# Output projection as seven half-size products (Strassen's scheme in Winograd's form) in a hybrid encoder layer

## The chip, the core and the metric

The kernel runs on one core of a Trainium2 chip. A core has five engines that run side by side, each in its own order, and wait for each other by semaphores: TensorE (PE; its weight loads are shown apart as PEld), VectorE (DVE), ScalarE (ACT), GpSimd (POOL) and SyncE (SP), which here issues all transfers between DRAM and the on-chip memory SBUF. TensorE writes its sums into PSUM, eight banks of 128 x 512 float32. The metric is the device time of one execution in microseconds (us); lower is better.

## What is computed

One layer on x of 2048 tokens by 2048 channels, float32. The condition c gives shift, scale and gate; the normalised input goes through one projection to 4096 columns; half the width is mixed by centred pooling windows, half by a recurrent unit in both directions; each half is normalised, gated and projected back, and the sum with x is normalised.

```python
mod = c_act @ w_ada[l] + b_ada[l]
shift, scale, gate = jnp.split(mod, 3, axis=-1)
h = rms_norm(x, norm_g[l]) * (1.0 + scale[:, None, :]) + shift[:, None, :]
z = h @ w_in[l] + b_in[l]
...
y_pool = rms_norm(y_pool, out_norm_pool_g[l]) * jax.nn.silu(g_pool)
y_lru = rms_norm(y_lru, out_norm_lru_g[l]) * jax.nn.silu(g_lru)
y = jnp.concatenate([y_pool, y_lru], axis=-1) @ w_out[l] + b_out[l]
x = x + gate[:, None, :] * y
return rms_norm(x, final_norm_g)
```

## The kernel before

All large products are made in two parts per operand: a float32 value is split into a rounded part and the rest (`m_split`, `w_split`, `y_split`: ScalarE copies, VectorE subtracts), and `mm3` adds three of the four part products. The work is a list of steps t. A step takes one moving operand M (256 rows of the sum by 512 columns, two parts) against four stationary tiles of 128, two halves of the sum and three part products: 24 matmuls into four PSUM banks.

Steps 0 to 255 are the input projection: eight groups of 256 channels, four token blocks of 512 each, eight steps to a sum. Beside them, at steps given by `at(step, function, ...)`, run the mixers of the groups that are ready (`lru_unit`, `pool_unit`), which leave y in DRAM (`yscr`) and the sums of squares of each half in `sq`; `rn` turns these into 1/rms.

Steps 256 to 383 are the output projection (`where2`): four token blocks (tb), four blocks of 512 output columns (dc), eight pairs p of 128 rows each. The y of a token block is loaded (`y_load`), multiplied by 1/rms and split (`y_split`) once, and stays in the eight buffers of pool `s` for the four column blocks. The blocks of w_out come in as M, one per step. When a sum is complete, `out_evac` multiplies the bank by the gate row, adds it to the row tile o (which holds x plus gate times b_out) and squares it; when all four column blocks are there, `out_row` makes 1/rms of the row, multiplies and stores.

What sets the order: the loop over t issues, for step t, the loads four steps ahead (`m_load`, `AHEAD`), the split of the operand for step t+2, the split of one w or y operand, the products of step t, then whatever `at` holds for t. The framework then orders the instructions of each engine by its own estimate, so the written order on VectorE is not the order of the code. Buffers come from pools that are used in turn: `raw` has 7 buffers for everything that is loaded and split, `m` has 3, `s` has 8; a load into a buffer waits on SP's queue until the buffer's last reader is done, and all loads behind it wait too. In the last four steps the products go tile by tile, so that a row's end can start while the next tile is still being summed.

```python
    def m_split(t):
...
        act(out=m[:, 0], in_=r, func=AF.Copy)
        vtt(out=m[:, 1], in0=r, in1=mf[:, 0], op=ALU.subtract)
```

## Time and profile before

| | |
|---|---|
| median of 3 runs | 2354.26 us (2354.2 to 2354.26) |
| span of the profiled execution, first to last instruction | 2352.7 us |
| granted TensorE clock, mean | 0.998 |
| PE, PEld, DVE, ACT, POOL busy | 99%, 82%, 65%, 54%, 0% |
| bytes moved | 437.09 MB, 186 GB/s on average |

The profiled execution has no run time of its own beside its span; the runs are 1.6 us longer than the span. The page gives busy shares of each engine, the same in 40 slices of the span, and the chain of work that ended last. The views of the trace list what an engine waited for, the mean duration of each group of instructions, the busy time in a stretch, and instructions in order of time. The input projection fills the span up to 1635 us, the output projection the rest.

### The profile page before, as it was taken

How to read it: one execution, taken by the hardware profiler on the slowest of the kernel's cores; microseconds unless marked ns; L12 is line 12 of the kernel's file. 1: busy time of each engine (PE TensorE's matmuls, PEld its weight loads, DVE VectorE, ACT ScalarE, POOL GpSimd, SP SyncE). 2: the span in 40 equal slices, each digit the busy share in tenths (PEclk: the TensorE clock that was granted, in tenths of full speed). 3: DMA queues.
4: the chain of work that ended last, by engine and by line, in shares of the span. 5: the costliest groups of instructions: out<-in, count | busy, mean ns of one | idle time of the engine just before them, and what ended most of it. 6: DMA issues, size and time to landing. Idle time of an engine off the chain costs nothing.

```text
span 2352.7 us, 26479 instructions
## 1 busy us (share of the span) xinstructions
PE 2330.4 (99%) x10216; PEld 1917.9 (82%) x10216; DVE 1524.7 (65%) x1898; ACT 1261.5 (54%) x1609; POOL 6.2 (0%) x40
## 2 busy tenths in 40 slices
PE   7999999999999999999999999999999999999998
PEld 6888888888888888888888888888788888888886
DVE  7999676567877555574764756569936636637535
ACT  4556686767656665665776566675323224224222
POOL 0000000000000000000000000000000000000000
PEclk9999999999999999999999999999999999999999
DMA  9889755345565634444363344446534634625531
GB/s 390 310 303 324 253 208 199 112 170 215 215 242 210 219 116 145 142 154 137 135 241 116 130 143 157 157 166 229 221 97 161 250 99 152 252 98 198 196 97 74
DMA packets 110655, 437.09 MB, mean 186 GB/s; under 512 B 12224, under 2 KB 13504, under 8 KB 100544
## 3 DMA queue, kind: packets, MB, share of 16 engines
q1 hardware_dynamic: 110528, 435.40, 52.0%
q8 instruction: 80, 1.31, 0.2%
q14 instruction: 47, 0.39, 0.1%
HBM read 358.80 MB, written 76.55 MB: 185 GB/s over the span
## 4 chain that ended last, share of the span: by engine, by line
PE 98%; DMA 1%; DVE 0%; SPq 0%; ACT 0%; issue 0%; DVEq 0%
PE pm L249 25%; PE pm L247 25%; PE pm L248 25%; PE px L247 7%; PE px L249 7%; PE px L248 7%; DMA ada<-in_wada_dram 1%; PE px L330 0%; DMA xr<-in_xc_dram 0%; PE px L644 0%; DVE ada L315 0%; DVE o L671 0%; SPq L274 0%; SPq L273 0%; PE px L212 0%; ACT s L225 0%
## 5 line engine op out<-in xcount | busy, mean ns | idle before, releaser
L247 PE MATMUL pm<-m,s 128*128 128x512 f32 x2638 | 1031.7, 391 | 0.0
L249 PE MATMUL pm<-m,s 128*128 128x512 f32 x2638 | 1027.0, 389 | 0.0
L248 PE MATMUL pm<-m,s 128*128 128x512 f32 x2638 | 1026.9, 389 | 0.0
L156 DVE TENSOR_TENSOR m<-xr,m 128x1024 fp32r<-128x1024 f32 x382 | 465.7, 1220 | 562.9 <-ACT m L155 557.7
L155 ACT ACTIVATE m<-xr 128x1024 fp32r<-128x1024 f32 x382 | 403.7, 1057 | 765.5 <-PE pm L249 607.7
L248 PEld LDWEIGHTS pm<-m,s 128*128 128x128 f32 x2638 | 495.4, 188 | 105.9 <-issue 2.2
L247 PEld LDWEIGHTS pm<-m,s 128*128 128x128 f32 x2638 | 495.3, 188 | 105.6 <-issue 2.6
L249 PEld LDWEIGHTS pm<-m,s 128*128 128x128 f32 x2638 | 495.2, 188 | 103.5
L247 PE MATMUL px<-m,s 128*128 128x512 f32 x426 | 164.6, 393 | 12.9 <-ACT m L296 12.5
L248 PE MATMUL px<-m,s 128*128 128x512 f32 x426 | 164.2, 391 | 0.0
L249 PE MATMUL px<-m,s 128*128 128x512 f32 x426 | 164.0, 391 | 0.0
L315 DVE CUSTOM_DVE_ANT_0 ada<-ada,cact 128x2048 f32<-128x2048 f32 x47 | 107.4, 2284 | 10.1 <-DMA ada<-in_wada_dram 10.1
L247 PEld LDWEIGHTS px<-m,s 128*128 128x128 f32 x426 | 80.1, 189 | 30.7 <-ACT m L296 12.5
L247 PE MATMUL px<-uch,gw 128*128 128x512 f32 x256 | 100.7, 394 | 0.0
L249 PE MATMUL px<-uch,gw 128*128 128x512 f32 x256 | 100.7, 393 | 0.0
L248 PE MATMUL px<-uch,gw 128*128 128x512 f32 x256 | 99.5, 389 | 0.0
L248 PEld LDWEIGHTS px<-m,s 128*128 128x128 f32 x426 | 80.4, 189 | 17.3 <-DVE m L297 0.4
L249 PEld LDWEIGHTS px<-m,s 128*128 128x128 f32 x426 | 80.4, 189 | 16.7
L476 DVE SCALAR_TENSOR_TENSOR th<-rg,th 128x512 f32<-128x512 f32 x64 | 42.7, 682 | 77.7 <-ACT th L471 77.6
L457 DVE TENSOR_TENSOR ig<-ig,u 128x512 f32<-128x512 f32 x64 | 44.2, 691 | 66.3 <-ACT ig L455 66.2
L656 ACT ACTIVATE ov<-o 128x512 f32<-128x512 f32 x64 | 39.9, 624 | 68.1 <-DVE o L655 68.1
L221 DVE TENSOR_TENSOR s<-wr,s 128x1024 fp32r<-128x1024 f32 x56 | 68.1, 1215 | 0.0
(166 smaller groups left out, 2069.2 us busy)
## 6 DMA issues: line engine op xcount, KB each, us to landing
xr<-xs SPq DMA_DIRECT2D x192, 512.0 KB, 4.8
xr<-in_wout_dram SPq DMA_DIRECT2D x128, 512.0 KB, 3.7
ada<-in_wada_dram SPq DMA_DIRECT2D x47, 1024.0 KB, 7.0
wr<-in_win_dram SPq DMA_DIRECT2D x71, 512.0 KB, 5.5
xr<-in_xc_dram SPq DMA_DIRECT2D x63, 512.0 KB, 6.1
gs<-gr SPq DMA_DIRECT2D x32, 512.0 KB, 3.1
xs<-xr SPq DMA_DIRECT2D x32, 512.0 KB, 3.7
gl<-gs SPq DMA_DIRECT2D x32, 512.0 KB, 3.5
```

Source lines behind the costliest of these rows:

```text
L155: act(out=m[:, 0], in_=r, func=AF.Copy)
L156: vtt(out=m[:, 1], in0=r, in1=mf[:, 0], op=ALU.subtract)
L221: vtt(out=s[:, 1], in0=r, in1=sf[:, 0], op=ALU.subtract)
L247: nc.tensor.matmul(out=ps, lhsT=a[:, 0, j, asl], rhs=b[:, 0, j], start=first, stop=False)
L248: nc.tensor.matmul(out=ps, lhsT=a[:, 0, j, asl], rhs=b[:, 1, j], start=False, stop=False)
L249: nc.tensor.matmul(out=ps, lhsT=a[:, 1, j, asl], rhs=b[:, 0, j], start=False, stop=last)
L315: nc.vector.tensor_tensor_reduce(out=t, in0=t, in1=cact["t"], op0=ALU.mult, op1=ALU.add, scale=1.0, scalar=0.0, accum_out=mod[:, i:i + 1])
L457: vtt(out=st["i", i], in0=st["i", i], in1=U[i][:, us], op=ALU.mult)
L476: stt(out=t, in0=a, scalar=1.0, in1=t, op0=ALU.add, op1=ALU.mult)
L656: act(out=v, in_=o[:, ds], func=AF.Square, accum_out=ssq[:, 4 * tb + t, dc:dc + 1])
```

## The change

The output projection is made by Strassen's scheme with Winograd's seven products. 1024 tokens (a group sg, two token blocks) by 2048 rows of the sum by 2048 columns are cut into halves in each direction: A11, A12, A21, A22 are the quarters of y (first index the token block, second the half of the channels) and B11 to B22 those of w_out. The products are A11 B11, A12 B21, S2 T2, S3 T3, A22 T4, S1 T1 and S4 B22, with S1 = A21 + A22, S2 = S1 - A11, S3 = A11 - A21, S4 = A12 - S2 and T1 = B12 - B11, T2 = B22 - T1, T3 = B22 - B12, T4 = T2 - B21. Each product has two column blocks q of 512 and four pairs p, 8 steps; a group has 56 steps and there are two groups, so the steps 256 to 367 stand where 256 to 383 stood. A step is the same 24 matmuls.

The combinations T1 to T4 are made during the input projection (`combine_load`, `combine`, `combine_store`, 32 times) and kept in DRAM. The quarters of y are loaded one unit after the other (`unit_load`, `unit_split`, one unit every two steps from step 249 on); a normalised quarter is written back to DRAM and loaded again where it is needed. `out_evac` copies or adds each product's bank into the tiles of `C_t`; product 1 is added onto the bank of product 0, and product 6 onto that of product 5, after these have been read (`CHAINED`). x is loaded in half rows (`x_load`), gate and b_out come in afterwards (`half_fin`, `part_fin`). `raw` has 8 buffers; the pools of the mixers are closed at step 262 and the rows of gate, b_out and final norm take their place. Comments were removed in the same edit.

```diff
-    raw_p = pool("raw", 7)
+    raw_p = pool("raw", 8)
...
+    mix_pools = [tc.alloc_tile_pool(name=n, bufs=b, side="right") for n, b in (("tmp", 9), ("gw", 1), ("uch", 1))]
+    tmp_p, gw_p, uch_p = mix_pools
...
+    tscr = [[[dram.tile([128, 2, TB], F32, name=f"t{k}_{p}_{q}") for q in range(2)] for p in range(4)] for k in range(4)]
+    sscr = [dram.tile([128, 2, TB], F32, name=f"ss{p}") for p in range(4)]
...
     NT1 = 256
-    NT = 384
+    SG = 56
+    NT = NT1 + 2 * SG
...
+    PRODUCTS = [("A11", "B11"), ("A12", "B21"), ("S2", "T2"), ("S3", "T3"), ("A22", "T4"), ("S1", "T1"), ("S4", "B22")]
+    CHAINED = {1: 0, 6: 5}
     def where2(t):
-        """Token block, column block, pair of a step of the output projection."""
-        i = t - NT1
-        return i // 32, i // 8 % 4, i % 8
-
-    # ---- operands: the exact two-part split of float32 ----
+        sg, i = divmod(t - NT1, SG)
+        return sg, i // 8, i // 4 % 2, i % 4
+    def wout_src(name, p, q):
+        k = int(name[1:])
+        if name[0] == "T":
+            return tscr[k - 1][p][q]
+        return wout[p + 4 * (k // 10 - 1), q + 2 * (k % 10 - 1)]
     S_t = {}
...
-            tb, dc, p = where2(t)
-            load(out=r, in_=wout[p, dc])
+            sg, k, q, p = where2(t)
+            load(out=r, in_=wout_src(PRODUCTS[k][1], p, q))
...
+    def combine_load(k, p, q):
...
+        a, b = (("B12", "B11"), ("B22", "T1"), ("B22", "B12"), ("T2", "B21"))[k]
+        for i, n in enumerate((a, b)):
+            r = raw("tr")
+            load(out=r, in_=wout_src(n, p, q))
+            wraw["t", k, i] = r
+    def combine(k, p, q):
+        a, b = wraw.pop(("t", k, 0)), wraw.pop(("t", k, 1))
+        vtt(out=a, in0=a, in1=b, op=ALU.subtract)
+        wraw["t", k] = a
+    def combine_store(k, p, q):
+        store(out=tscr[k][p][q], in_=wraw.pop(("t", k)))
...
+    def unit_args(u):
+        sg, u = divmod(u, 28)
+        return sg, PRODUCTS[u // 4][0], u % 4
+    def unit_load(u):
+        sg, name, p = unit_args(u)
+        ya, yb = ([yscr[PAIRS[k]][2 * sg + h] for k in (p, p + 4)] for h in range(2))
+        srcs = {"A11": [ya[0]], "A12": [ya[1]], "S2": [yb[0], yb[1], ya[0]], "S3": [ya[0], yb[0]], "A22": [yb[1]],
+                "S1": [yb[0], yb[1]], "S4": [ya[1], sscr[p]]}[name]
+        yraw[u] = []
+        for src in srcs:
+            r = raw("yr")
+            load(out=r, in_=src)
+            yraw[u].append(r)
+    def normed(r, sg, h, k, p):
+        for j in range(2):
+            vtt(out=r[:, j], in0=r[:, j], in1=rn_t[2 * sg + h, "PL"[k]], op=ALU.mult)
+        late.append((yscr[PAIRS[p + 4 * k]][2 * sg + h], r))
+        if (sg, h, p) == (0, 1, 3):
+            del rn_t[1, "PL"[k]], rn_t[0, "PL"[k]]
+    def unit_split(u):
+        sg, name, p = unit_args(u)
+        rs = yraw.pop(u)
+        r = rs[0]
+        if name in ("A11", "A12"):
+            normed(r, sg, 0, int(name[2]) - 1, p)
+        elif name == "S2":
+            r = rs[2]
+            normed(rs[0], sg, 1, 0, p)
+            normed(rs[1], sg, 1, 1, p)
+            vtt(out=r, in0=r, in1=rs[0], op=ALU.subtract)
+            vtt(out=r, in0=rs[1], in1=r, op=ALU.subtract)
+            late.append((sscr[p], r))
+        elif name in ("S3", "S4"):
+            vtt(out=r, in0=r, in1=rs[1], op=ALU.subtract)
+        elif name == "S1":
+            vtt(out=r, in0=r, in1=rs[1], op=ALU.add)
         s = s_p.tile([128, 2, 2, TB], F32R, tag="s", name="s")
-        sf = s.bitcast(F32)
-        rn = sq[GROUPS[PAIRS[p]][0]][:, tb * TB:(tb + 1) * TB]
-        for j in range(2):
-            vtt(out=r[:, j], in0=r[:, j], in1=rn, op=ALU.mult)
         act(out=s[:, 0], in_=r, func=AF.Copy)
-        vtt(out=s[:, 1], in0=r, in1=sf[:, 0], op=ALU.subtract)
-        S_t[8 + tb, p] = s
...
+    def mm3(ps, a, asl, b, j, first, last, more=False):
+        for i, (x, y) in enumerate(((0, 0), (0, 1), (1, 0))):
+            nc.tensor.matmul(out=ps, lhsT=a[:, x, j, asl], rhs=b[:, y, j], start=first and i == 0, stop=last and i == 2,
+                             skip_group_check=more)
...
+    def step(bk, sk, p, m, tiles, first, last, by_j=False, more=False):
...
+    def rows_open():
...
+        for p in reversed(mix_pools):
+            p.release()
+        row_p = ctx.enter_context(tc.tile_pool(name="row", bufs=1, side="right", reuse_waits="tile"))
+        for n in ("gb", "fg", "gate"):
+            fin[n] = row_p.tile([128, D], F32, tag=n, name=n)
...
+        for i, (tb, kind) in enumerate([(2, "P"), (2, "L"), (3, "P"), (3, "L")]):
+            act(out=fin["rn"][:, i], in_=rn_t[tb, kind], func=AF.Copy)
+            rn_t[tb, kind] = fin["rn"][:, i]
+        sq.clear()
...
+    def out_evac(sg, k, q, banks, tiles):
+        lo, hi = (slice((q + 2 * h) * TB, (q + 2 * h + 1) * TB) for h in range(2))
+        for n in tiles:
+            for i, at_k in ((n, 0), (n + 4, 3)):
+                if k == at_k and q == 0:
+                    C_t[sg, i] = big("o")[:, :D]
+            a, b, ps = C_t[sg, n], C_t.get((sg, n + 4)), banks[n]
+            if k == 0:
+                act(out=a[:, hi], in_=ps, func=AF.Copy)
+            elif k == 1:
+                act(out=a[:, lo], in_=ps, func=AF.Copy)
+            elif k in (2, 6):
+                vtt(out=a[:, hi], in0=ps, in1=a[:, hi], op=ALU.add)
+            elif k == 3:
+                vtt(out=b[:, hi], in0=ps, in1=a[:, hi], op=ALU.add)
+            elif k == 4:
+                vtt(out=b[:, lo], in0=b[:, hi], in1=ps, op=ALU.subtract)
+            else:
+                vtt(out=b[:, hi], in0=ps, in1=b[:, hi], op=ALU.add)
...
+        x_t[sg, n, h] = r
+    def x_add(sg, n, h):
+        r = x_t[sg, n, h]
+        vtt(out=r, in0=r, in1=fin["gb"][:, h * 1024:(h + 1) * 1024], op=ALU.add)
+    def part_fin(sg, n, h, lo, hi, slot):
+        r = x_t[sg, n, h][:, lo:hi]
+        ds = slice(h * 1024 + lo, h * 1024 + hi)
+        o = C_t[sg, n][:, ds]
+        vtt(out=o, in0=o, in1=fin["gate"][:, ds], op=ALU.mult)
+        vtt(out=o, in0=o, in1=r, op=ALU.add)
+        act(out=r, in_=o, func=AF.Square, accum_out=ssq[:, row_of(sg, n), slot:slot + 1])
+        if hi == 1024:
+            del x_t[sg, n, h]
+    def half_fin(sg, n, h):
+        x_add(sg, n, h)
+        part_fin(sg, n, h, 0, 1024, h)
+    def out_row(sg, n, slots, parts):
+        i = row_of(sg, n)
+        o = C_t.pop((sg, n))
         s = ssq[:, i]
         r = rst[:, i:i + 1]
-        vtt(out=s[:, 0:1], in0=s[:, 0:1], in1=s[:, 1:2], op=ALU.add)
-        vtt(out=s[:, 0:1], in0=s[:, 0:1], in1=s[:, 2:3], op=ALU.add)
...
+    for i in range(32):
+        q, k = divmod(i, 4)
+        b = 68 + 5 * i if i < 7 else 134 + (i - 7) * 9 // 2
+        at(b, combine_load, k, q // 2, q % 2)
+        at(b + 2, combine, k, q // 2, q % 2)
+        at(b + 3, combine_store, k, q // 2, q % 2)
...
+    for sg in range(2):
+        b = NT1 + SG * sg
+        for n in range(4):
+            step_b = (49 + 2 * n, 49 + n)[sg]
+            for i, h, e in ((n, 0, b + 22 + 2 * n), (n + 4, 0, b + 41 + 2 * n), (n + 4, 1, b + step_b)):
+                at(e - 2, x_load, sg, i, h)
+                at(e, half_fin, sg, i, h)
+            at(b + 50 + n, x_load, sg, n, 1)
+            if sg == 0:
+                at(b + 52 + n, x_add, sg, n, 1)
+                at(b + 56 + n, part_fin, sg, n, 1, 0, 1024, 1)
+                at(b + 56 + n, out_row, sg, n, 2, 1)
+                at(b + 61 + n, out_row, sg, n + 4, 2, 1)
+            else:
+                at(b + 50 + n, out_row, sg, n + 4, 2, 1)
+                e = b + min(52 + n, 54)
+                at(e, x_add, sg, n, 1)
+                at(e, part_fin, sg, n, 1, 0, TB, 1)
...
+    rn_at = [(244, 1, "L"), (244, 2, "L"), (245, 3, "L"), (245, 0, "P"), (249, 1, "P"), (250, 0, "L"), (254, 2, "P"), (259, 3, "P")]
...
+    unit_at = {}
+    for u in range(56):
+        unit_at[max(NT1 - 10 + 2 * u, NT1 - 7 + u)] = u
...
-            key = (8 + tb, dc)
-            sk = 8 + tb
+            sg, k, q, p = where2(t)
+            key = (8 + sg, CHAINED.get(k, k), q)
+            sk = (8 + sg, PRODUCTS[k][0])
...
+        for dst, src in late:
+            store(out=dst, in_=src)
+        late.clear()
...
+        if t + W_AHEAD in unit_at:
+            unit_load(unit_at[t + W_AHEAD])
...
+        if t in unit_at:
+            unit_split(unit_at[t])
...
-                out_evac(tb, dc, bk, range(4))
-                if dc == 3:
-                    for i in range(4):
-                        at(t + 2 + i, out_row, tb, i, 1)
+                out_evac(sg, k, q, bk, range(4))
             else:
                 for i in range(4):
-                    for q in range(4, 8):
-                        step(bk, sk, q, M_t[t - 7 + q], (i,))
-                    out_evac(tb, dc, bk, (i,))
-                    out_row(tb, i, 4 if i == 3 else 2)
-        # the rest
```

On VectorE, at the border of two token blocks before (splits for steps 323 to 325): m is the moving operand, s and yr the operand made of y, o a row tile, `fg` the row of the final norm.

```order
L156 TENSOR_TENSOR m_14252<-xr_14164,m_14252 128x1024
L242 TENSOR_TENSOR s_14255<-yr_14166,s_14255 128x1024
L665 TENSOR_TENSOR rst_101<-ssq_100 128x1 x4
L667 RECIPROCAL rst_101<-rst_101 128x1
L671 SCALAR_TENSOR_TENSOR o_13285<-o_13285,rst_101,fg_12049 128x2048
L156 TENSOR_TENSOR m_14290<-xr_14200,m_14290 128x1024
L667 RECIPROCAL rst_101<-rst_101 128x1 x3
L671 SCALAR_TENSOR_TENSOR o_13324<-o_13324,rst_101,fg_12049 128x2048
L671 SCALAR_TENSOR_TENSOR o_13363<-o_13363,rst_101,fg_12049 128x2048
L156 TENSOR_TENSOR m_14326<-xr_14250,m_14326 128x1024
L671 SCALAR_TENSOR_TENSOR o_13395<-o_13395,rst_101,fg_12049 128x2048
```

and at the border of the two token groups in the changed kernel (splits for steps 320 and 321), where `rn` holds 1/rms, and the three yr are the quarters of an S2 operand:

```order
L170 TENSOR_TENSOR m_14627<-xr_14539,m_14627 128x1024
L280 TENSOR_TENSOR yr_14542<-yr_14542,rn_12524 128x512
L280 TENSOR_TENSOR yr_14544<-yr_14544,rn_12524 128x512 x2
L295 TENSOR_TENSOR yr_14546<-yr_14546,yr_14542 128x1024
L769 TENSOR_TENSOR rst_101<-ssq_100 128x1
L296 TENSOR_TENSOR yr_14546<-yr_14544,yr_14546 128x1024
L771 RECIPROCAL rst_101<-rst_101 128x1
L775 SCALAR_TENSOR_TENSOR o_13329<-o_13329,rst_101,fg_12520 128x2048
L304 TENSOR_TENSOR s_14636<-yr_14546,s_14636 128x1024
L170 TENSOR_TENSOR m_14673<-xr_14584,m_14673 128x1024
```

The row normalisations by `fg` stood next to each other between splits and now stand among the products and differences of the S2 operand, nine rows between two splits.

On VectorE, the end before, from the bank of the third tile on (px and pm are PSUM banks):

```order
L654 TENSOR_TENSOR ov_16379<-px_16162,gate_12051 128x512
L655 TENSOR_TENSOR o_15571<-o_15571,ov_16379 128x512
L665 TENSOR_TENSOR rst_101<-ssq_100 128x1
L667 RECIPROCAL rst_101<-rst_101 128x1
L671 SCALAR_TENSOR_TENSOR o_15571<-o_15571,rst_101,fg_12049 128x1024 x2
L654 TENSOR_TENSOR ov_16416<-pm_16163,gate_12051 128x512
L655 TENSOR_TENSOR o_15603<-o_15603,ov_16416 128x512
L665 TENSOR_TENSOR rst_101<-ssq_100 128x1
L667 RECIPROCAL rst_101<-rst_101 128x1
L671 SCALAR_TENSOR_TENSOR o_15603<-o_15603,rst_101,fg_12049 128x512 x4
```

and the end of the changed kernel, from the bank of the fourth tile on:

```order
L725 TENSOR_TENSOR o_14530<-pm_16036,o_14530 128x512
L775 SCALAR_TENSOR_TENSOR o_14526<-o_14526,rst_101,fg_12520 128x1024 x2
L769 TENSOR_TENSOR rst_101<-ssq_100 128x1
L753 TENSOR_TENSOR o_14530<-o_14530,gate_12521 128x512
L771 RECIPROCAL rst_101<-rst_101 128x1
L769 TENSOR_TENSOR ssq_100<-ssq_100 128x1
L754 TENSOR_TENSOR o_14530<-o_14530,x_16341 128x512
L775 SCALAR_TENSOR_TENSOR o_14528<-o_14528,rst_101,fg_12520 128x1024 x2
L769 TENSOR_TENSOR rst_101<-ssq_100 128x1
L771 RECIPROCAL rst_101<-rst_101 128x1
L775 SCALAR_TENSOR_TENSOR o_14530<-o_14530,rst_101,fg_12520 128x512 x4
```

Before, a tile's half rows (L671) stood ahead of the next tile's bank; now the half rows of the second and third tile (L775 on o_14526 and o_14528) stand behind the bank of the fourth.

## Rows read from the trace of the kernel before

**Rows 1.** Page: busy time and share by engine, and the granted clock in 40 slices.
```profile
PE 2330.4 (99%) x10216; PEld 1917.9 (82%) x10216; DVE 1524.7 (65%) x1898; ACT 1261.5 (54%) x1609; POOL 6.2 (0%) x40
...
PEclk9999999999999999999999999999999999999999
```
**Rows 2.** Waits of TensorE: who waited for whom, us in total, times, longest.
```profile
PE px L247 <- ACT m L296: 12.5, 1, 12.5
```
**Rows 3.** Page: the chain that ended last, by engine.
```profile
PE 98%; DMA 1%; DVE 0%; SPq 0%; ACT 0%; issue 0%; DVEq 0%
```
**Rows 4.** Timeline of VectorE late in the kernel: start us, us, line, operation, tiles.
```profile
2284.42 1.23 DVE L156 TENSOR_TENSOR m<-xr,m 128x1024 fp32r<-128x1024 f32 x1 [4.21 <-ACT m L155]
2289.86 1.23 DVE L156 TENSOR_TENSOR m<-xr,m 128x1024 fp32r<-128x1024 f32 x1 [4.21 <-ACT m L155]
```
**Rows 5.** Timeline of ScalarE, same stretch; in brackets idle before, and its end.
```profile
2310.58 1.06 ACT L155 ACTIVATE m<-xr 128x1024 fp32r<-128x1024 f32 x1 [4.38 <-PE pm L249]
```
**Rows 6.** Groups of VectorE by line and shape: busy, mean ns, idle before.
```profile
L156 DVE TENSOR_TENSOR m<-xr,m 128x1024 fp32r<-128x1024 f32 x382 | 465.7, 1220 | 562.9 <-ACT m L155 557.7 <-DMA o<-in_xn_dram 4.2 <-issue 0.3
...
L671 DVE SCALAR_TENSOR_TENSOR o<-o,rst,fg 128x2048 f32<-128x2048 f32 x12 | 27.9, 2348 | 0.1
...
L240 DVE TENSOR_TENSOR yr<-yr,sqL 128x512 f32<-128x512 f32 x32 | 21.1, 686 | 20.7 <-DMA yr<-ys 20.7
...
L240 DVE TENSOR_TENSOR yr<-yr,sqP 128x512 f32<-128x512 f32 x32 | 20.7, 686 | 26.9 <-DMA yr<-ys 26.9
...
L332 DVE RECIPROCAL sqP<-sqP 128x512 f32<-128x512 f32 x4 | 13.4, 3346 | 0.8 <-ACT sqP L331 0.8
```
**Rows 7.** Timelines of VectorE and TensorE around the start of step 266.
```profile
1692.74 1.28 DVE L655 TENSOR_TENSOR o<-o,ov 128x512 f32<-128x512 f32 x2
...
1699.60 2.29 DVE L156 TENSOR_TENSOR m<-xr,m 128x1024 fp32r<-128x1024 f32 x2
...
1701.05 0.62 PE L247 MATMUL px<-m,s 128*128 128x512 f32 x2
```
**Rows 8.** Stretches: busy us of PE, PEld, DVE, ACT, POOL; clock, DMA share, GB/s.
```profile
1635.00:2321.00 686.00, 686.00 (x3009) 564.46 (x3009) 380.19 (x438) 208.39 (x297) 0.00 (x0) 1.00 0.46 160
...
1657.16:1700.75 43.59, 43.59 (x181) 33.77 (x180) 43.29 (x28) 13.77 (x21) 0.00 (x0) 1.00 0.47 180
...
0.00:40.00 40.00, 27.09 (x106) 21.25 (x107) 28.29 (x39) 18.49 (x21) 0.44 (x6) 1.00 0.97 378
```
**Rows 9.** Chain of waits in order of time: the sum over partitions for 1/rms.
```profile
1604.31 0.86 PE px L330 x2
```
**Rows 10.** Transfers by tiles: count, KB each, median us from issue to landing.
```profile
xr<-in_xc_dram SPq DMA_DIRECT2D x63, 512.0 KB, 6.1
...
yr<-ys SPq DMA_DIRECT2D x32, 512.0 KB, 3.3
```
**Rows 11.** Waits of SP's queue: us in total, times, longest.
```profile
SPq L140 <- DVE m L156: 359.4, 77, 16.2
```
**Rows 12.** Timeline of VectorE at the end, from the last tile's bank on.
```profile
2340.82 2.48 DVE L671 SCALAR_TENSOR_TENSOR o<-o,rst,fg 128x1024 f32<-128x1024 f32 x2
2343.39 0.69 DVE L654 TENSOR_TENSOR ov<-pm,gate 128x512 f32<-128x512 f32 x1
2344.12 0.69 DVE L655 TENSOR_TENSOR o<-o,ov 128x512 f32<-128x512 f32 x1
2345.59 0.16 DVE L665 TENSOR_TENSOR rst<-ssq 128x1 f32<-128x1 f32 x1 [0.79 <-ACT ov L656]
...
2346.31 2.74 DVE L671 SCALAR_TENSOR_TENSOR o<-o,rst,fg 128x512 f32<-128x512 f32 x4
```
**Rows 13.** Page: the costliest groups: line, tiles, count, busy us, mean ns.
```profile
L247 PE MATMUL pm<-m,s 128*128 128x512 f32 x2638 | 1031.7, 391 | 0.0
...
L247 PE MATMUL px<-m,s 128*128 128x512 f32 x426 | 164.6, 393 | 12.9 <-ACT m L296 12.5
```

More of the change, by code (lines that the diff above doesn't have):

```diff
@@ L251, in step @@
-    def step(bk, sk, p, m, tiles, by_j=False):
+        vtt(out=s[:, 1], in0=r, in1=s.bitcast(F32)[:, 0], op=ALU.subtract)
+        S_t[(8 + sg, name), p] = s
+    def mm3(ps, a, asl, b, j, first, last, more=False):
[3 more added lines that the diff above has]
+    def step(bk, sk, p, m, tiles, first, last, by_j=False, more=False):
@@ L252, in step @@
         s = S_t[sk, p]
         for n, j in [(n, j) for j in range(2) for n in tiles] if by_j else [(n, j) for n in tiles for j in range(2)]:
-            mm3(bk[n], s, slice(n * 128, (n + 1) * 128), m, j, p == 0 and j == 0, p == 7 and j == 1)
+            mm3(bk[n], s, slice(n * 128, (n + 1) * 128), m, j, first and j == 0, last and j == 1, more)
     ada_t = {}
@@ L643, in gate_rows @@
         ps = px()
-        nc.tensor.matmul(out=ps, lhsT=ones, rhs=t[:, :TB], start=True, stop=True)
-        nc.vector.tensor_copy(fin["gate"][:, i * TB:(i + 1) * TB], ps)
+        nc.tensor.matmul(out=ps, lhsT=ones, rhs=t, start=True, stop=True)
+        act(out=fin["gate"][:, i * TB:(i + 1) * TB], in_=ps, func=AF.Copy)
         if i == 3:
             vtt(out=fin["gb"], in0=fin["gb"], in1=fin["gate"], op=ALU.mult)
-    def out_evac(tb, dc, banks, tiles):
-        ds = slice(dc * TB, (dc + 1) * TB)
-        for t in tiles:
-            v = tmp("ov")[:, :TB]
-            o = o_t[tb, t]
-            vtt(out=v, in0=banks[t], in1=fin["gate"][:, ds], op=ALU.mult)
-            vtt(out=o[:, ds], in0=o[:, ds], in1=v, op=ALU.add)
-            act(out=v, in_=o[:, ds], func=AF.Square, accum_out=ssq[:, 4 * tb + t, dc:dc + 1])
@@ new lines, in layer, with row_of, x_load @@
+    x_t = {}
+    def row_of(sg, n):
+        return 8 * sg + n
+    def x_load(sg, n, h):
+        r = raw("x").rearrange("p j t -> p (j t)")
+        i = row_of(sg, n)
+        load(out=r, in_=xn[i * 128:(i + 1) * 128, h * 1024:(h + 1) * 1024])
+        x_t[sg, n, h] = r
[11 more added lines that the diff above has]
+            del x_t[sg, n, h]
@@ L661, in out_row @@
+    def half_fin(sg, n, h):
+        x_add(sg, n, h)
+        part_fin(sg, n, h, 0, 1024, h)
+    def out_row(sg, n, slots, parts):
+        i = row_of(sg, n)
+        o = C_t.pop((sg, n))
         s = ssq[:, i]
         r = rst[:, i:i + 1]
-        vtt(out=s[:, 0:1], in0=s[:, 0:1], in1=s[:, 1:2], op=ALU.add)
-        vtt(out=s[:, 0:1], in0=s[:, 0:1], in1=s[:, 2:3], op=ALU.add)
-        vtt(out=r, in0=s[:, 0:1], in1=s[:, 3:4], op=ALU.add)
+        for k in range(1, slots):
+            vtt(out=r if k == slots - 1 else s[:, 0:1], in0=s[:, 0:1], in1=s[:, k:k + 1], op=ALU.add)
@@ L804, in layer @@
         e = t - 25
-        if e >= 0 and e % 32 < 8:
-            if e // 32 < 7:
-                w_split(e // 32 + 1, e % 32)
-            elif e // 32 < 11:
-                y_split(e // 32 - 7, e % 32)
-        if p == 0:
+        if 0 <= e < 224 and e % 32 < 8:
+            w_split(e // 32 + 1, e % 32)
+        if t in unit_at:
+            unit_split(unit_at[t])
+        if key not in banks:
             if t == 0:
@@ L814, in layer @@
             else:
-                banks[key] = [px(), px(), px(), pm()] if t >= NT1 and dc % 2 else [pm() for _ in range(4)]
+                banks[key] = [px(), px(), px(), pm()] if t >= NT1 and q else [pm() for _ in range(4)]
         bk = banks[key]
         if t < NT - 4:
-            step(bk, sk, p, M_t.pop(t), range(4), t == 0)
-        if t < NT - 4 and (t >= NT1 and dc == 3 or t < NT1 and tb == 3):
+            step(bk, sk, p, M_t.pop(t), range(4), first, last, t == 0, t >= NT1 and k in CHAINED)
+        if t < NT - 4 and (t >= NT1 and q or t < NT1 and tb == 3):
             del S_t[sk, p]
-        if p == 7:
-            del banks[key]
+        if last:
+            if t < NT1 or k not in CHAINED.values():
+                del banks[key]
             if t < 32:
@@ L827, in layer @@
             elif t < NT - 1:
-                out_evac(tb, dc, bk, range(4))
-                if dc == 3:
-                    for i in range(4):
-                        at(t + 2 + i, out_row, tb, i, 1)
+                out_evac(sg, k, q, bk, range(4))
             else:
                 for i in range(4):
-                    for q in range(4, 8):
-                        step(bk, sk, q, M_t[t - 7 + q], (i,))
-                    out_evac(tb, dc, bk, (i,))
-                    out_row(tb, i, 4 if i == 3 else 2)
+                    for p_ in range(4):
+                        step(bk, sk, p_, M_t[t - 3 + p_], (i,), False, p_ == 3, more=True)
+                    out_evac(sg, k, q, bk, (i,))
+                    part_fin(sg, i, 1, TB, 2 * TB, 2)
+                    out_row(sg, i, 3, 4 if i == 3 else 2)
         for u in units:
```

63 lines of the change are left out of this document (18 added, 45 removed).

## The prediction, before the changed kernel ran

> **What bounds the kernel now.** I read the page first. TensorE is busy 99% of the span at a full granted clock, VectorE 65%, ScalarE 54% [rows 1]; the reader is to see that one engine is full from end to end and the others are not. The list of what TensorE waited for says the same more sharply: one wait of 12.5 us at the very start and nothing else worth a microsecond [rows 2]. The chain of waits that ends last is TensorE for 98% [rows 3]. So the time before is a sum of matmuls, plus about 22 us around them, and only two things can move it: fewer matmuls, or a wait that appears where there is none now.
>
> The price of a matmul comes from the rhythm of the steps. The subtraction that splits one 512-column operand starts every 5.44 us late in the kernel (2284.42, 2289.86) [rows 4]. A step issues 4 x 2 x 3 = 24 matmuls, so one costs 0.2267 us.
>
> **What the change removes.** The output projection goes from 128 steps to 2 x 56 = 112. Sixteen steps of 24 matmuls are 384 matmuls fewer, and the instruction order shows exactly that (9812 against 10196). 16 x 5.44 = 87.0 us. Nothing hid this work and nothing replaces it on TensorE: the input projection, the mixers, the sums for 1/rms and the rows of the gate issue the same matmuls as before. This term is the safest of all.
>
> **How late an operand may be.** The split of step n needs one of three M buffers, free when step n-3 ends; ScalarE's copy (1.06) is seen to wait for TensorE before it [rows 5], and VectorE's subtraction takes 1.22 [rows 6]. Step n begins two steps after that, so an operand that VectorE handles at once comes 10.88 - 1.06 - 1.22 = 8.6 us early. VectorE works strictly in its written order in this trace, so whatever stands in front of a split eats from these 8.6 us, and only beyond them does TensorE wait.
>
> **VectorE's load.** I counted its instructions from the order of the changed kernel. Durations: 128x1024 1.15 and 128x512 0.64, each taken back to back [rows 7], 128x2048 2.35 and the reciprocal 3.35 [rows 6]; 512-wide ones with a scalar are a little longer, so mixed groups are taken at 0.68. In the output projection there are 285 of 1024, 136 of 512, 11 of 2048 and a few small ones, about 460 us in 110 steps of 598 us: 77%. Before, it was 380 of 686, 55% [rows 8]. On average there is room, so the question is the dense places.
>
> Densest place before: from 1657.16 to 1700.75 VectorE is busy 43.29 of 43.59 us [rows 8], and the split for step 266 ends at about 1700.76, while its first matmul starts at 1701.05 [rows 7]. TensorE did not wait. Eight full steps with no gap can therefore be borne, just.
>
> - Start of the output projection (splits of steps 248 to 255): 13 x 1.15 + 4 x 3.35 + 43 x 0.68 = 57.6 us. TensorE's 8 steps give 43.5, the three sums for 1/rms 3 x 0.86 [rows 9], 12 matmuls of the mixer 2.7: 48.8. The excess is 8.8 against 8.6 spare. Bounds: 0, because the scheduler has placed the splits between the long ones and the old place held too; 6, if the waits for ScalarE's square roots come on top. I take 2.
> - Border between the two token groups (splits of steps 309 to 320): the eight row normalisations of the first group (8 x 2.35), 32 x 1.15, 20 x 0.64 and small ones are 70.8 us in 65.3. The excess is 5.5 of 8.6. In the same stretch the new S2 operands begin, and each operand that is normalised now waits for its load: 20.7 + 26.9 us over 32 of them before, 1.5 each [rows 6]. Six of those would take 9 us more. Bounds 0 and 10; I take 2.5, nearer to the row of the old dense place, which had such waits too.
> - Evacuation itself: before, a bank cost two passes of VectorE and one of ScalarE; now products 0 and 1 are copied by ScalarE and the other five cost one pass of VectorE. It lies beside the products, with four steps until the bank is needed again, and I price it at nothing; it is inside the counts above.
>
> **The transfers.** At the border I count, for steps 313 to 327, 45 transfers of 0.524 MB and 8 rows of 1.05 MB: 32.0 MB in 15 x 5.44 = 81.6 us, 392 GB/s. In its first 40 us the trace moves 378 GB/s at a DMA share of 0.97 [rows 8]. At that rate the stretch needs 84.7 us, 3 us more than it has; the spare time of the operands covers that, so it costs nothing by itself and only adds to the upper bound of the border.
>
> Under a rate like that first stretch a 512 KB load of x lands in 6.1 us, against 3.3 for the loads of y in the old output projection [rows 10]. The Trainium skill ("DMA: Bandwidth & Descriptors", section Specifications) gives about 358 GB/s as a core's HBM limit, under a fabric ceiling of 435. By 358 the stretch would take 89.4 us and be 7.8 us late, which with the 5.5 above is more than 8.6, and the border would cost about 5 instead of 2.5. The row shows 378 GB/s sustained, so the trace is above the page's limit, and I keep to the row.
>
> **The combinations of w_out.** 32 subtractions of 1.22 are 39 us of VectorE beside the input projection, where it has 1524.7 - 380 = 1145 us of work in 1635 [rows 1, 8]. Each brings two loads and a store (96 x 0.524 = 50 MB) and holds two raw buffers for two steps, one of them for a step and a store more. SP issues in order and already waits for a raw buffer at most loads of x: 359.4 us in 77 waits, the longest 16.2 [rows 11]; all of that is hidden today. The pool grows from 7 to 8 buffers. Bounds 0 and 6 (three combinations fall in steps 90 to 101, the busiest of that stage); I take 1.
>
> **The end.** Before, from the first instruction after the last product to the last output instruction is 2343.39 to 2349.05, 5.66 us: product, sum, square, root, and four quarter rows of 2.74 [rows 12]. In the new order VectorE handles, behind the last product's bank, in this sequence: its sum from PSUM (0.73), the two half rows of tile 1 (2.48), the gate product (0.73), the sum with x (0.73), the two half rows of tile 2 (2.48), three small ones (3 x 0.16), the root's latency (0.72) and 2.74. That is 11.1, so the end grows by 5.4. Half rows of two earlier tiles have slid behind the last bank because the sums of tiles 1 and 2 are written in front of them and wait for TensorE. Bounds 4.5 and 6.5 (ScalarE hidden or not). The last operand is also split later than before, but 14 matmuls of the next tile are written in front of it; I price that at nothing, 2 at most, inside the upper bound.
>
> **The sum.** 2352.7 - 87.0 + 5.4 + 2 + 2.5 + 1 = 2276.6 span. The runs' median of 2354.26 is 1.6 above this execution's span, so 2278 as a time of a run.
>
> **Rivals.**
> - B, the S2 operands make a queue of their own. Each needs three loads where an old one needed one, and the third is issued only when a split two steps earlier has freed its buffer. If each load leaves 1.5 us uncovered, as before [rows 6], 8 operands x 3 x 1.5 = 36 us, less 8.6 of spare in each of the two groups: 19 us, 2297. For it: 392 GB/s and SP in order. Against it: loads are issued two steps ahead, and VectorE has 5 x 1.15 + 4 x 0.64 = 8.3 us of work in 10.88 there.
> - C, everything is covered, the end included: 2352.7 - 87.0 + 1.6 = 2267. Against it: the order at the end is fixed.
> - D, slower. The combinations hold raw buffers in the input projection; SP, in order, issues the next operand behind a combination's store, and TensorE waits in a stage where it never did. It decides from (2354 - 2278)/32 = 2.4 us per combination. A whole step each would be 174 us: 2452. For it: the 359.4 us of SP waits. Against it: those are hidden with 7 buffers, and only 0.45 of a buffer a step is asked for more (50 in the 112 steps from 134 on), with 8 of them.
> - E, the saving doesn't come: the matmuls of the seven products run slower (two of them add to a bank that is being read), and 2688 x 0.2267 grows by 14% (87/609). Same time as before, 2354. Nothing in the trace speaks for it: matmuls into the two pools of banks take the same time, 391 and 393 ns [rows 13].
>
> **Chances.** My forecast (2270 to 2288) 0.68; B 0.24 (2288 to 2312); C 0.03; D 0.03; E 0.02. About 0.2%, 4.7 us, is what can be told from no change. Faster 0.95, same 0.01, slower 0.04. The range 2269 to 2298 holds the forecast and half of B.
>
> **What would show it.** TensorE's matmul count is 9832 in the trace (10216 - 384) and its pace 5.44 a step; if the pace differs, E. Waits of TensorE beyond the first 12.5 us lie near steps 248 to 256 and 316 to 328; if they add to over 12 us, B, and the engine before them tells whether VectorE's own work or a load of y ended them. From the last matmul to the end of the span it is about 15 us, 9.3 before. In the input projection TensorE should show no wait; one there, ended by a split behind a late load, is D.

## The result and the profile after

The changed kernel takes 2274.83 us (median of 4 runs, 2274.06 to 2274.89) beside 2354.26 us before (2354.2 to 2354.45): a ratio of 0.9662, 95% interval 0.9648 to 0.9675. The forecast was 2278, in a range of 2269 to 2298. The profiled execution has a span of 2272.7 us, 80.0 less than before. In line numbers of the changed kernel, L310 is `mm3`, L169 and L170 are the operand's split, L280 to L304 `unit_split`, L725 the evacuation of the seventh product, L746 to L755 sum with x, gate and squares, L775 the output rows.

The page first, busy time by engine and the granted clock in 40 slices:

```profile
PE 2241.9 (99%) x9832; PEld 1845.5 (81%) x9832; DVE 1656.3 (73%) x1986; ACT 1294.4 (57%) x1609; POOL 6.2 (0%) x40
...
PEclk9999999999999999999999999999999999999998
```

TensorE has 9832 matmuls, 384 fewer than in [rows 1], at the same clock but for the last slice, in which it has finished. VectorE has 132 us more to do. The waits of TensorE and the chain that ended last answer to [rows 2, 3] (who waited for whom: us in total, times, longest):

```profile
PE px L310 <- ACT m L359: 12.4, 1, 12.4
PE px L310 <- DVE m L170: 0.7, 1, 0.7
...
PE px L310 <- DVE uch L624: 0.2, 1, 0.2
```
```profile
PE 95%; DVE 3%; DMA 1%; issue 0%; ACT 0%; SPq 0%; DVEq 0%
```

There is still one long wait, the one at the start. No operand of the new output projection held TensorE up until the last product, where the split of the last operand but one comes 0.7 us late. What has changed in the chain is that VectorE is now 3% of it, 72 us. About half of that is the end, from 2230 us on. Nearly all the rest is the dense start of the output projection, from 1573 to 1612 us, which ends in the wait of 0.2 us for `uch`, an operand of the mixers. These are stretches of the trace (from : to, us, busy us of PE, PEld, DVE, ACT, POOL; clock, DMA share, GB/s): the border of the token groups (splits 309 to 320), steps 313 to 327, and the time after the last matmul:

```profile
1927.70:1993.00 65.30, 65.30 (x290) 54.09 (x289) 64.73 (x73) 29.80 (x44) 0.00 (x0) 1.00 0.88 316
...
1955.30:2036.90 81.60, 81.60 (x361) 67.59 (x361) 68.11 (x74) 34.66 (x48) 0.00 (x0) 1.00 0.93 354
...
2256.00:2272.70 16.70, 0.00 (x0) 0.00 (x0) 12.55 (x22) 2.33 (x7) 0.00 (x0) 0.57 0.64 252
```

At the border VectorE is busy 64.73 of 65.30 us, and TensorE 65.30 of 65.30. The end answers to [rows 12]: the last matmuls, of the kernel before and of the changed one, and VectorE behind them in the changed one (start us, us, line, operation, tiles; in brackets idle time before):

```profile
2342.96 0.40 PE L249 MATMUL pm<-ml,s 128*128 128x512 f32 x1
```
```profile
2254.41 1.56 PE L310 MATMUL pm<-ml,s 128*128 128x512 f32 x6
```
```profile
2255.53 2.47 DVE L775 SCALAR_TENSOR_TENSOR o<-o,rst,fg 128x1024 f32<-128x1024 f32 x2
...
2258.72 0.68 DVE L725 TENSOR_TENSOR o<-pm,o 128x512 f32<-128x512 f32 x1
2259.32 2.47 DVE L775 SCALAR_TENSOR_TENSOR o<-o,rst,fg 128x1024 f32<-128x1024 f32 x2
...
2263.12 2.47 DVE L775 SCALAR_TENSOR_TENSOR o<-o,rst,fg 128x1024 f32<-128x1024 f32 x2
...
2266.21 2.74 DVE L775 SCALAR_TENSOR_TENSOR o<-o,rst,fg 128x512 f32<-128x512 f32 x4
```

The last matmul ends at 2254.41 + 1.56 = 2255.97. VectorE reads that bank only at 2258.72, 2.75 us later, and its last instruction ends at 2268.95. Before, the last matmul ended at 2343.36 and VectorE read the bank at 2343.39. So the span is made of three pieces: 12.4 us before the first matmul (12.5 before), 2243.6 us from there to the last (2330.8 before, 87.2 less), and 16.7 us behind it (9.3 before, 7.4 more). -0.1 - 87.2 + 7.4 = -80.0 with rounding.

### The profile page after: what moved, and what is told of

Read it like the earlier page. It is cut to its first block, busy times and chain, and to the rows that moved or that the text cites. A ratio compares the mean times of both kernels' runs of the same rounds, so it can differ in the third digit from the quotient of the medians.

```text
span 2272.7 us, 26096 instructions
## 1 busy us (share of the span) xinstructions
PE 2241.9 (99%) x9832; PEld 1845.5 (81%) x9832; DVE 1656.3 (73%) x1986; ACT 1294.4 (57%) x1609; POOL 6.2 (0%) x40
## 4 chain that ended last, share of the span: by engine, by line
PE 95%; DVE 3%; DMA 1%; issue 0%; ACT 0%; SPq 0%; DVEq 0%
PE pm L310 75%; PE px L310 20%; DVE o L775 1%; DMA ada<-in_wada_dram 1%; DMA xr<-in_xc_dram 0%; PE px L393 0%; DVE sqP L395 0%; DVE m L170 0%; DVE o L754 0%; DVE o L753 0%; DVE sqL L395 0%; DVE o L725 0%; PE px L707 0%; DVE x L746 0%; DVE th L549 0%
## 5 line engine op out<-in xcount | busy, mean ns | idle before, releaser
L310 PE MATMUL pm<-m,s 128*128 128x512 f32 x7674 | 1771.0, 390 | 0.0
L310 PEld LDWEIGHTS pm<-m,s 128*128 128x128 f32 x7674 | 1440.8, 188 | 304.0 <-issue 4.1
L169 ACT ACTIVATE m<-xr 128x1024 fp32r<-128x1024 f32 x366 | 386.4, 1056 | 587.0 <-PE pm L310 396.8
L170 DVE TENSOR_TENSOR m<-xr,m 128x1024 fp32r<-128x1024 f32 x366 | 446.2, 1219 | 359.8 <-ACT m L169 348.1
L310 PE MATMUL px<-m,s 128*128 128x512 f32 x1134 | 270.7, 392 | 13.8 <-ACT m L359 12.4
L310 PEld LDWEIGHTS px<-m,s 128*128 128x128 f32 x1134 | 213.6, 189 | 60.3 <-ACT m L359 12.4
L310 PE MATMUL px<-uch,gw 128*128 128x512 f32 x768 | 186.8, 391 | 0.0
L310 PEld LDWEIGHTS px<-uch,gw 128*128 128x128 f32 x768 | 144.3, 188 | 31.5 <-ACT sqL L394 0.5
L303 ACT ACTIVATE s<-yr 128x1024 fp32r<-128x1024 f32 x56 | 59.0, 1053 | 46.3 <-DVE yr L299 21.8
L304 DVE TENSOR_TENSOR s<-yr,s 128x1024 fp32r<-128x1024 f32 x56 | 68.2, 1218 | 12.3 <-ACT s L303 12.2
L185 ACT ACTIVATE xr<-xr,shv 128x512 f32<-128x512 f32 x64 | 44.3, 719 | 34.2 <-DVE xr L184 29.5
L755 ACT ACTIVATE x<-o 128x1024 f32<-128x1024 f32 (+1 forms) x36 | 34.7, 965 | 50.6 <-DVE o L754 49.1
L234 ACT ACTIVATE s<-wr 128x1024 fp32r<-128x1024 f32 x56 | 58.6, 1046 | 3.8 <-PE pm L310 2.0
L499 DVE SCALAR_TENSOR_TENSOR cv<-u,vec,cv 128x512 f32<-128x512 f32 x64 | 45.8, 743 | 6.7 <-ACT cv L497 6.7
L518 ACT ACTIVATE ig<-px,vec 128x512 f32<-128x512 f32 x64 | 43.7, 683 | 10.7 <-PE px L310 10.2
```

The lines of the kernel that those rows point to most:

```text
L185: act(out=r[:, j], in_=r[:, j], func=AF.Identity, bias=shv[:, k:k + 1])
L234: act(out=s[:, 0], in_=r, func=AF.Copy)
L303: act(out=s[:, 0], in_=r, func=AF.Copy)
L304: vtt(out=s[:, 1], in0=r, in1=s.bitcast(F32)[:, 0], op=ALU.subtract)
L310: nc.tensor.matmul(out=ps, lhsT=a[:, x, j, asl], rhs=b[:, y, j], start=first and i == 0, stop=last and i == 2, skip_group_check=more)
L499: stt(out=a if k < 3 else U[i][:, us], in0=src, scalar=cw, in1=a, op0=ALU.mult, op1=ALU.add)
```

## The experiments

Each was timed beside the kernel before, whose median was 2354.4 to 2354.6 us each time. Theory from the trace: the 384 matmuls bring their full time, what was added in the middle is covered, and VectorE's work at the end gives 7.4 us back. Rivals: the matmuls bring less and something else gained; the covered parts cost something unseen; at the end it is the order, not the amount.

**1. The 384 matmuls alone.** In the kernel before:

```diff
-            step(bk, sk, p, M_t.pop(t), range(4), t == 0)
+            m = M_t.pop(t)
+            if t < NT1 or p != 3:
+                step(bk, sk, p, m, range(4), t == 0)
```

> The kernel before, with the 24 matmuls of one step in eight of the output projection (pair 3 of every column block) left out, so its rows lack an eighth of that sum; the operands of these steps are still loaded and split. It prices the 384 matmuls alone. Forecast's theory (TensorE is full, a matmul is 0.2267 us): 2354.3 - 87.0 = 2267.2 us, within 1 us, and the rest of the change then costs about 7.5 us. Rival (the 16 steps were partly covered by something else, and the rest of the change gave part of the gain): less than 80 us saved, above 2274.

Measured: 2272.13 us (2270.59 to 2272.19), 82.3 us less than before. Between the two predictions, nearer to the full price. The missing 4.7 us are nearly all in one place, seen in the waits of TensorE and in stretches around it (columns as above):

```profile
PE px L248 <- DVE m L156: 2.3, 1, 2.3
```
```profile
1698.00:1700.00 2.00, 1.10 (x3) 0.91 (x4) 2.00 (x3) 0.00 (x0) 0.00 (x0) 0.77 0.02 4
1700.00:1702.00 2.00, 2.00 (x6) 1.54 (x6) 2.00 (x2) 1.06 (x1) 0.00 (x0) 0.50 0.88 289
1702.00:1704.00 2.00, 2.00 (x9) 1.64 (x8) 2.00 (x2) 0.00 (x0) 0.00 (x0) 0.87 0.98 344
```

It is the dense place of [rows 7, 8], where the split for step 266 ended 0.3 us ahead of the step's first matmul. With fewer matmuls beside the same VectorE work the cover is gone: TensorE waits 2.3 us, and then runs some 3 us at a granted clock of 0.50, half speed. So the matmuls are worth 87 us only as long as VectorE's dense places keep up. In the changed kernel the split for step 266 ends 5.5 us ahead of the step, and that kernel gets the full 87.2.

**2. Without the combinations.** `wout_src` returns plain blocks for T1 to T4, and the three `at` lines of the combinations are gone.

> The changed kernel without the 32 combinations beside the input projection: four of the seven products read plain blocks of w_out instead, so the output lacks the combinations on that side. 96 transfers and 39 us of VectorE's work are gone. Theory now (TensorE saw no wait in the input projection, so the combinations cost nothing): 2274.8, within 0.5 us. The prediction's own term: 1 us less, 2273.8. Rival (each combination holds up TensorE a little, in a way that the list of waits hides): 3 us less or more, 2271.8 or below.

Measured: 2275.11 us (2274.49 to 2275.7), no difference from 2274.83. As they stand, the combinations cost nothing that can be told from the spread of these runs, about 1 us.

**3. Combinations four times as heavy.**

```diff
+        for _ in range(3):
+            vtt(out=b, in0=b, in1=b, op=ALU.max)
         vtt(out=a, in0=a, in1=b, op=ALU.subtract)
```

> The changed kernel with three more VectorE instructions of 128x1024 (the maximum of a block with itself, which leaves it as it was) ahead of each of the 32 combinations: 32 x 3 x 1.15 = 110 us more on VectorE beside the input projection. Theory (a delay costs only what is over an operand's spare time; the smallest spare in the input projection is 1.9 us at step 98 and 2.1 at step 130, elsewhere 4 to 16): 0 to 4 us, 2274.8 to 2279. Rival D (what a combination adds stands in the path of the operands): 2.4 us or more for each, 32 x 3.45 = 110 us, 2385.

Measured: 2282.83 us (2281.81 to 2287.26), 8.0 us more. Of 110 us of extra work 102 were covered, so D is far off; but the theory's 4 us were exceeded too. The waits show why (the two added lines make `mm3` L312 here):

```profile
PE px L312 <- DVE uch L507: 3.0, 4, 0.9
PE px L312 <- DVE uch L626: 1.7, 4, 0.8
```

These eight are for `uch`, the mixers' own operands (a ninth, of 0.5 us, is for the reading of a bank), and none is for an M split. The spare time that I had counted, of the M splits, was not what ran out first.

**4. Seven raw buffers.** `raw_p = pool("raw", 7)`.

> The changed kernel with 7 raw buffers in place of 8, as before the change. Theory (loads are issued far enough ahead; the combinations and the S2 operands ask for less than the eighth buffer gives): same within 1 us, 2274 to 2276. Rival B/D (raw buffers and SP's order are what the change leans on): waits of TensorE at the S2 operands, steps 270 to 275 and 326 to 331, or beside the combinations, 5 us or more, 2280 and above.

Measured: 2283.03 us (2281.57 to 2285.84), 8.2 us more. The theory that the eighth buffer hardly matters is wrong. TensorE's waits from 2000 to 2100 us, and SP's issues at the border (start us, us from the first to the last of a group, line, tiles, count):

```profile
PE px L310 <- DVE m L170: 1.5, 2, 0.8
PE pm L310 <- ACT m L169: 0.9, 1, 0.9
PE pm L310 <- DVE m L170: 0.3, 1, 0.3
```
```profile
2022.35 0.33 SPq L157 DMA_DIRECT2D xr<-in_wout_dram  x1
2023.48 1.97 SPq L275 DMA_DIRECT2D yr<-ys  x3
2031.08 0.33 SPq L157 DMA_DIRECT2D xr<-in_wout_dram  x1
```

Two loads of the moving operand (L157) that should follow each other by a step of 5.44 us are 8.7 apart: three loads for an S2 operand stand between them, and then a buffer is missing. What SP waits for from 2005 to 2040 us is first of all the write-back of normalised quarters, which holds their buffers:

```profile
SPq L157 <- DMA ys<-yr: 9.6, 3, 4.1
```

Up to 2020 the stretches show fewer matmuls too, 9 from 20 to 1500 us and 9 from 1500 to 1700 (6503 and 853, against 6512 and 862 with eight buffers), 2 us each; from 2020 to 2050 there are 116 against 134, 4.1 us. So half of the loss lies beside the input projection and its end, half at the border. The kernel before was not run with eight buffers; its TensorE had no wait that they could have saved [rows 2].

**5. Seven buffers, no combinations**, experiments 2 and 4 together, to tell the two places apart.

> The changed kernel with 7 raw buffers and without the 32 combinations (plain blocks of w_out in place of the combined ones, so the output lacks the combinations on that side). With 7 buffers and the combinations it took 2283.0, 8.2 us more than with 8, and TensorE's waits lay in two places: about 5 us beside the input projection and 3.4 us at steps 327 to 330. Theory (the combinations need the eighth buffer beside the input projection, the S2 operands at the border): the waits of the input projection go, those of the border stay, 2277 to 2280. Rival 1 (7 buffers are too few for the new output projection alone, and its changed order reaches back): nothing goes, 2282 to 2284. Rival 2 (the combinations' transfers were what made the border late): all goes, 2275.

Measured: 2278.95 us (2278.66 to 2280.63), 4.1 us below experiment 4 and 4.1 above the changed kernel. From 20 to 1500 us there are 6513 matmuls again. The loss that is left is the border's:

```profile
PE px L310 <- ACT m L169: 1.2, 1, 1.2
PE px L310 <- DVE m L170: 0.8, 1, 0.8
```
```profile
2026.00:2028.00 2.00, 0.84 (x3) 0.19 (x1) 0.53 (x1) 1.06 (x1) 0.00 (x0) 1.00 0.98 399
2028.00:2030.00 2.00, 1.25 (x4) 1.01 (x5) 2.00 (x4) 0.00 (x0) 0.00 (x0) 0.88 0.37 70
2030.00:2032.00 2.00, 2.00 (x6) 1.61 (x5) 2.00 (x3) 0.00 (x0) 0.00 (x0) 0.50 0.74 207
```

Waits of 2.0 us, and again a stretch at clock 0.50 behind them. So the eighth buffer, which the change brings along, pays 4.1 us for the combinations and 4.1 for the border.

**6. More VectorE work at the border.**

```diff
         vtt(out=m[:, 1], in0=r, in1=mf[:, 0], op=ALU.subtract)
+        if 309 <= t <= 320:
+            vtt(out=m[:, 1], in0=r, in1=mf[:, 0], op=ALU.subtract)
```

> The changed kernel with VectorE's subtraction of the operand split done twice (the same result) for steps 309 to 320, at the border of the two token groups: 12 x 1.15 = 13.8 us more on VectorE, in a stretch where it is busy 64.73 of 65.30 us already. Theory (an operand may be some 8 us late before TensorE waits, and what is over costs its full length): 13.8 - 8 = 5.8 us, 2278 to 2283. Rival (the spare time is not there, the prediction's upper bound for the border was near): 10 us or more, 2285 and above. Second rival (VectorE catches up between, the spare is larger than thought): under 2 us.

Measured: 2280.96 us (2280.03 to 2283.64), 6.1 us more. The number is the theory's, but partly by luck. In the changed kernel only 5.0 us were left at the end of this stretch and not some 8: the split for step 321 ends 5.0 us ahead of the matmul that reads it. And the edit did more than add: the framework put two of the eight row normalisations behind the stretch. From the split of step 309 to that of step 321 VectorE takes 77.98 us, where it took 68.69: 9.3 us more, not 13.8. Less the 5.0 to spare that is 4.3, and TensorE lost 4.5 us at steps 317 to 319. The profiled execution, 5.1 us longer than that of the changed kernel, lost 1.4 us more around step 328, behind the doubled splits. Its new waits, 4.3 us, are for the operand's copy and its two subtractions (L169 to L172), the largest of them:

```profile
PE px L312 <- DVE m L172: 3.2, 2, 1.6
```
```profile
1990.00:1994.00 4.00, 2.53 (x12) 1.75 (x10) 4.00 (x4) 1.66 (x2) 0.00 (x0) 1.00 1.00 339
```

So an operand could be late by its spare time at no cost here, and what was over cost about its length; the granted clock stayed at 1.00.

**7. Five loads for each S2 operand.**

```diff
-        srcs = {... "S2": [yb[0], yb[1], ya[0]], ...
+        srcs = {... "S2": [yb[0], yb[1], ya[0], yb[0], yb[1]], ...
```

> The changed kernel with five loads in place of three for each S2 operand (two of its blocks are loaded a second time into buffers of their own and not used): 16 transfers of 0.524 MB more, eight of them in some 44 us beside steps 321 to 328. Theory (at 8 raw buffers the loads of S2 have little over: with 7 TensorE waited there): two buffers more held for two steps are like two fewer in the pool, 4 us or more at each of the two places, 2282 to 2295. Rival (the transfers' rate decides, not the buffers: 28.9 MB of 81.6 us plus 4.2 MB at the 384 GB/s seen there are 4.6 us late, within the spare time): 2274 to 2276. B as the prediction had it (1.5 us uncovered a load): 16 x 1.5 = 24 us, 2299.

Measured: 2283.91 us (2282.66 to 2285.07), 9.1 us more: the buffers' theory, but only in the second group, around step 327. SP's issues there, TensorE, and one stretch behind its wait:

```profile
2017.64 0.33 SPq L157 DMA_DIRECT2D xr<-in_wout_dram  x1
2018.85 11.84 SPq L275 DMA_DIRECT2D yr<-ys  x5
...
2033.06 0.33 SPq L157 DMA_DIRECT2D xr<-in_wout_dram  x1
```
```profile
2033.92 1.29 PE L310 MATMUL pm<-m,s 128*128 128x512 f32 x5
2039.08 6.97 PE L310 MATMUL px<-m,s 128*128 128x512 f32 x18 [3.86 <-ACT m L169]
```
```profile
2040.00:2042.00 2.00, 1.96 (x5) 1.38 (x5) 0.29 (x1) 0.00 (x0) 0.00 (x0) 0.50 1.03 420
```

The five loads take SP 11.84 us, since they wait for buffers, and the next moving operand is issued 15.4 us after the one before. TensorE waits 3.86 us, and its next 18 matmuls take 6.97 us where 18 take 4.24 elsewhere. This is the mechanism of rival B. The first group does not show it, so the price of 1.5 us a load was wrong (16 added loads would be 24 us). The second group had less to spare without the added loads too: in the changed kernel the split for step 329 ends only 1.5 us ahead of the matmul that reads it, the least of the output projection up to its last product, against 5.1 at step 270 in the first group. Buffers and transfer rate cannot be told apart fully here: the added loads raise both.

**8. Another order at the end.** The rows of the last tile are written ahead of those of the two tiles before it.

```diff
-                    out_row(sg, i, 3, 4 if i == 3 else 2)
+                    if i == 0:
+                        out_row(sg, 0, 3, 2)
+                for i in (3, 1, 2):
+                    out_row(sg, i, 3, 4 if i == 3 else 2)
```

> The changed kernel with the half rows of the third output tile of the end (and most of what belongs to the second) written behind the last tile's quarter rows; nothing is left out. Theory now (VectorE has no time free at the end: it takes the last bank 2.75 us after the last matmul and is busy 12.55 of the 12.95 us from then to its last instruction, so no order of the same instructions ends sooner): 2274 to 2276. Rival, the prediction's reading (what costs is that half rows stand behind the last bank, so moving them takes the 5.4 us back): 2269 to 2272.

Measured: 2274.61 us (2274.3 to 2276.18), no difference. VectorE:

```profile
2257.75 0.69 DVE L725 TENSOR_TENSOR o<-pm,o 128x512 f32<-128x512 f32 x1
...
2262.68 5.13 DVE L775 SCALAR_TENSOR_TENSOR o<-o,rst,fg 128x512 f32<-128x512 f32 x6
```

The half rows of the third tile now stand behind the quarter rows of the last (four quarters and two halves in one run), and VectorE ends at 2267.8 after a last matmul at 2255.2: 12.6 us against 13.0.

**9. Less VectorE work at the end.** In `out_evac` for the second group, and with `x_early` 12 to 16 steps ahead of the old place:

```diff
+            elif k == 6 and sg:
+                vtt(out=ps, in0=ps, in1=fin["gate"][:, hi], op=ALU.mult)
+                vtt(out=a[:, hi], in0=a[:, hi], in1=ps, op=ALU.add)
+                act(out=ps, in_=a[:, hi], func=AF.Square, accum_out=ssq[:, row_of(sg, n), 1 + q:2 + q])
...
+    def x_early(sg, n):
+        x_add(sg, n, 1)
+        r = x_t.pop((sg, n, 1))
+        o = C_t[sg, n][:, 1024:]
+        vtt(out=o, in0=o, in1=fin["gate"][:, 1024:], op=ALU.mult)
+        vtt(out=o, in0=o, in1=r, op=ALU.add)
...
```

> The changed kernel with less VectorE work at the end of the second token group, nothing left out: x and bias are added, and the part of the tile known before the seventh product is multiplied by the gate, 12 steps earlier; behind the last product a bank then takes two VectorE passes (product with the gate in place in its bank, sum) and not three, and x + bias is no longer there. About 9.7 us less VectorE work in the last 60 us. Theory (VectorE's work at the end is what the end costs): the last bank is taken at once and the chain behind it is 5.7 us and the 3.7 us of the store: 9.4 in place of 16.7 us from the last matmul on, 2267 to 2269. Rival (the order of the half rows, or the stores, set the end): 2273 to 2275. Second rival (the work moved into steps 348 to 354 makes operands late there): a wait of TensorE in that stretch, 2270 or more.

Measured: 2268.89 us (2268.72 to 2269.36), ratio to before 0.9637 (0.9624 to 0.965), 5.9 us less than the changed kernel and the best of all. The last matmul ends at 2255.92. VectorE (L786 is the output rows here, L725 the product with the gate):

```profile
2255.12 2.48 DVE L786 SCALAR_TENSOR_TENSOR o<-o,rst,fg 128x1024 f32<-128x1024 f32 x2
2257.52 0.69 DVE L725 TENSOR_TENSOR pm<-pm,gate 128x512 f32<-128x512 f32 x1
...
2260.44 2.74 DVE L786 SCALAR_TENSOR_TENSOR o<-o,rst,fg 128x512 f32<-128x512 f32 x4
```

From the last matmul to the end of the span it is now 2266.6 - 2255.92 = 10.7 us, 6.0 less. The last bank is still taken 1.6 us late, behind half rows of the third tile: that is about what is missing from the 9.4 expected. From 2240 us on VectorE has 20.23 us of work in place of 28.55, 8.3 less, and TensorE has no wait where the work went. With experiment 8 this points one way: at the end the amount of VectorE work counted, and one other order of it gained nothing.

## Why the prediction was right, point by point

- **The matmuls, -87.0.** Right: 384 fewer, and 87.2 us less from the first to the last. Experiment 1 adds what the step left out: alone, the missing matmuls give 82.3, since the old dense place cannot follow. Rival E is out, since the pace held: 18 matmuls take 4.24 us in a product that begins a bank (step 316, at 1971.66) as in one that is added onto it (step 327):

```profile
2031.50 4.24 PE L310 MATMUL px<-m,s 128*128 128x512 f32 x18
```

- **The spare time of an operand, 8.6 us.** Incomplete as a bound for the input projection, where the mixers' operands have less (experiment 3). Right in size, as a split with nothing in front of it shows: in the kernel before, VectorE's subtraction for step 270 ends at 1714.45, 8.6 us ahead of the matmul that reads it:

```profile
1713.22 1.23 DVE L156 TENSOR_TENSOR m<-xr,m 128x1024 fp32r<-128x1024 f32 x1 [4.17 <-ACT m L155]
```
```profile
1723.04 0.39 PE L248 MATMUL px<-m,s 128*128 128x512 f32 x1
```

- **Start of the output projection, +2.** Mis-sized: 0.2. VectorE's work was counted well: it took 57.1 us from the split of step 248 to that of step 256, where 57.6 were expected. But the first of these splits was 16.0 us ahead and not 8.6, and at the tightest 6.9 were left (step 253). What came late, by 0.2 us at 1612, was `uch` of the mixers, which this term did not look at.
- **Border, +2.5.** Mis-sized: 0, no wait of TensorE stands there. The instructions were counted exactly (8 of 2048, 32 of 1024, 20 of 512), but lasted 68.7 us and not 70.8, so they ate 3.4 us of the spare time and not 5.5. I had priced an excess below the spare at more than nothing, by the nearness to an old place that did not wait either [rows 7]; the lower bound was the right reading. The operand nearest to being late, of step 329, lies behind this stretch, beside the S2 loads (experiment 7).
- **Transfers, 0.** Right for the forecast. Steps 313 to 327 moved 354 GB/s where I had counted 392: 28.9 MB, so part of the 32.0 fell outside these steps. TensorE did not wait there, so they cost nothing. The Trainium skill ("DMA: Bandwidth & Descriptors", section Specifications) has about 358 GB/s as the limit, by which the prediction's estimate for the border was 5; the first 40 us of this trace move 379, beside 378 in [rows 8], so the trace stays above it.
- **The combinations, +1.** 0 (experiment 2), but only by the eighth buffer: with seven they cost 4.1 us.
- **The end, +5.4.** The step that failed in part: it grew by 7.4, 2.0 more, outside the bounds of 4.5 to 6.5. What stood behind the last bank was counted within 0.9 us (11.1 expected, 2268.95 - 2258.72 = 10.2 measured). Missed was that VectorE comes to this bank 2.75 us late, since it is busy without a break from 2240 to 2256. The two partly cancel, which is luck. The step also named the order of the half rows as the reason; experiment 8 moves them and gains nothing.
- **The rivals.** B (2297) did not happen, but its mechanism is the nearest to happening: one buffer fewer, or two loads more for each S2 operand, bring it about, at 4 and 9 us and not 19. C had all covered, the end included: true of everything but the end. D would have needed 2.4 us per combination, and even 3.45 us more of VectorE on each cost 0.25.

The sum was 2276.6 for the span and came out at 2272.7: 5.5 us too much in the middle, 2.0 too little at the end, 0.3 in the matmuls and the start.
